# Computing 64 instead of 32 expert tiles of the first table ahead, with the gate matrix built beside 56 of them

## The chip, the core and the metric

The kernel runs on one core of a Trainium2 chip. TensorE (PE) multiplies matrices, VectorE (DVE) and ScalarE (ACT) work element by element, GpSimd (POOL) here starts the row gathers, and SyncE (SP) starts all other transfers. The engines run side by side, each in its own fixed order, and wait for each other by semaphores. The metric is the device time of one launch in microseconds (us); the figure shown is the median of a few runs.

## What is computed

One decoder layer on 512 tokens of width 2048, in float32. The first half (two kinds of linear attention, projections, norms) is untouched here. The second half is PEER, a layer of 16384 single-neuron experts, of which each token uses 128:

```
qry = xt @ w_query                     # 8 heads x 256
s1, s2 = qry halves @ sub_keys         # scores against 128 + 128 keys
v1, i1 = top_k(s1, 16); v2, i2 = top_k(s2, 16)
best, pos = top_k(v1[:, None] + v2[None, :], 16)
expert = i1[pos // 16] * 128 + i2[pos % 16]
gate = softmax(best)
hid = gelu(x . u_tab[expert])          # 128 experts of each token
y = sum(gate * hid * v_tab[expert])
out = rmsnorm(h + y)
```

## The kernel before

The kernel splits the 512 tokens. For 352 of them (`TD`) all 16384 experts are computed densely, and a gate matrix that is zero outside the chosen experts picks the right ones. For the other 160 tokens the chosen rows are gathered from both tables: 320 transfers of 128 rows, 1 MB each.

The dense part runs in 128 tiles of 128 experts and 32 groups of 4 tiles:

- **A tile of the first table** (`u_steps`, L1107): two half-tiles of 512 KB are loaded by SP (`wr`), cast by ACT to a high part `wh` (L100), and DVE subtracts to get the low part `wl` (L102, 128x1024). 48 matmuls of 352 columns follow (L239 to L241, into `lin`). DVE multiplies by the norm (`hid`, L1118, 352 columns) and ACT applies Gelu.
- **A group of the second table** (`v_chunk`, L1151): 8 chunks, each with one `wr` load, one `wh`, one `wl` on DVE and 24 matmuls (L1163 to L1165), whose two results DVE adds to `hT` (L1166, 352 columns). So a group has 8 `wl`, 192 matmuls and 16 additions.
- **The weights of a group** (`w_alloc` L1129, `w_make` L1137): the group's piece of the gate matrix is loaded into `gm` (one buffer, 704 KB); for each of the 4 tiles DVE makes `wf` from `hid` and `gm` (L1142), ACT casts it to `wgh`, DVE makes `wgl` (L1144). The next `gm` load can start when the fourth `wf` has read the buffer.
- **The gate matrix** (`gate_block`, L1073) is built in 88 blocks. For every two blocks DVE runs four 128x1024 operations (L1090 to L1093, tiles `oa`, `ob`); each block has 8 small matmuls (L1100) and one copy on ACT. Every 8 blocks, 2 MB go to DRAM (`gd`).
- **The gather** (`gather_steps`, L1198): POOL starts an indirect transfer into `row` (3 buffers). For a row of the first table DVE multiplies and sums (L1218, 128x2048), for a row of the second it multiplies and adds (L1231, 128x2048). There are 160 of each.

The order is written out in `peer` (L839). (1) While the top-16 indices are worked out, 8 tiles are computed and spilled to DRAM (`hidd`). (2) The *gate stage* computes the next `left = 4*NP1 - et` tiles, spills them, and spreads the 88 blocks evenly over them. (3) The *mixed stage* takes the groups from `NP1` on: for each, 4 tiles of the first table are computed in line, beside the 8 chunks of the group before. (4) The *second-table stage* takes the first `NP1` groups: their `hid` comes back from DRAM (L1148), and only chunks of the second table are computed.

The gather is paced by `tick` (L926), called after each tile, and after each quarter of a group's chunks:

```
slots = 4 * (2 * NG - NP1) + EARLY * 4 * NP1 - 16
self.slot += share
want = int(len(self.steps) * min(self.slot / slots, 1.0))
```

A tick in stages 3 and 4 counts 1, in stages 1 and 2 `EARLY`. The scheduler then fixes each engine's order from this text, and may move a step ahead where it finds room.

Of the kernel before, what the change touches and what calls it, by code (L numbers as in the profile page):

```python
# [42 lines left out]
ND = NC_ - 1  # L43
QS = P // EX
SL = P // QS
NP1 = 8
TS = 8
TB = 32
LAG = 8
X1, X2 = 6, 12  # L50
QW, YL, WAIT = 12, 5, 7
RATE_B, RATE_A, OWED = 1.8, 5.0, 6.0
EARLY = 0.2
GSC = 32768.0


# [21 lines left out]
class Kernel:  # L78
# [760 lines left out]
    def peer(self):  # L839
# [4 lines left out]
        with pool("dp") as self.dp:  # L844
            with pool("tr") as self.trp:
                with pool("tk") as self.tk:
# [23 lines left out]
                    with pool("tk2") as self.fp:  # L870
# [3 lines left out]
                        for n, c in enumerate(list(range(ND, NC_)) + list(range(ND))):  # L874
                            self.pick(c)
                            for _ in range(2):
                                self.u_spill(et)
                                et += 1
                                if self.trs:
                                    self.tick(EARLY)  # L880
                                for _ in soft:
                                    pass
                            self.place(c)
                with pool("tk3") as self.fp:
# [4 lines left out]
                    self.gn = 0  # L889
                    left = 4 * NP1 - et  # L890
                    done = 0
                    for n in range(2 * left):
# [7 lines left out]
                        if n % 2:  # L900
                            hid = next(u)
                            nc.sync.dma_start(self.hidd[et // 4, :, et % 4], hid)
                            et += 1
                            self.tick(EARLY)
            with pool("fo") as self.fop, pool("fq") as self.fp:
                order = list(range(NP1, NG)) + list(range(NP1))
                w, wn = None, None
                self.vn = 0
                for n in range(NG + 1):
                    g = order[n] if n < NG else None  # L910
                    self.vtags = ("g", "g", "g", "s") if n < NG - NP1 else ("g", "s", "lin", "g", "lin", "g", "lin")
                    if g is not None:
                        wn = self.w_alloc(g)
                    for e in range(4):
                        if g is not None:
                            self.w_make(*wn, e, self.u_tile(4 * g + e) if g >= NP1 else self.hid_load(g, e))
                            if g >= NP1:
                                self.tick()
# [7 lines left out]
    def tick(self, share=1.0):  # L926

        slots = 4 * (2 * NG - NP1) + EARLY * 4 * NP1 - 16
        self.slot += share
# [416 lines left out]
```

## Time and profile before

| | before |
|---|---|
| median of 3 runs | 3552.33 us (3538.89 to 3554.91) |
| the profiled execution's own time | 3555.49 us |
| its span | 3553.7 us |
| PE busy | 3333.5 us (94%) |
| DVE busy | 2765.4 us (78%) |
| ACT busy | 1206.4 us (34%) |
| bytes read from and written to HBM | 748.73 MB, 38.09 MB |

The span is the time from the first to the last instruction that the trace has; the own time also has what lies around it. Busy shares are averages over stages with different limits, so the stages are read one by one.

### The profile page before, as it was taken

The page shows a single profiled execution, that of the slowest core. Times are in us where ns is not written, and L with a number is a line of the kernel's source. Part 1 is how long each engine was busy: PE and PEld are TensorE (multiplying, and loading weights), DVE is VectorE, ACT ScalarE, POOL GpSimd, SP SyncE. Part 2 cuts the span into 40 slices and gives each one's busy share as a digit, 9 for nine tenths or more (in the row PEclk, how much of TensorE's full clock was granted, in tenths as well). Part 3 has the DMA queues.
Part 4 walks back from the last instruction along what each step waited for, and adds up shares of the span by engine and source line. Part 5 has one row for each costly group of instructions (what it writes and reads, how often), then busy time and mean ns, then how long its engine had stood idle before and what let it go on. Part 6 is the DMA issues. An engine that isn't in the chain of part 4 may idle for free.

```text
span 3553.7 us, 49698 instructions
## 1 busy us (share of the span) xinstructions
PE 3333.5 (94%) x19740; PEld 3091.5 (87%) x19740; DVE 2765.4 (78%) x4095; ACT 1206.4 (34%) x1499; POOL 873.0 (25%) x533
## 2 busy tenths in 40 slices
PE   7889899999999996888899999999999999999997
PEld 5667678888788996888899999999999999999997
DVE  7666654444534679999899999899899999998666
ACT  5333432322332212355433333333233333333334
POOL 4232223333354230000122222222222222321000
PEclk9889989999999998899999999999999999999999
DMA  4232322222432223556699999999999999998553
GB/s 150 75 92 88 89 60 78 84 77 80 141 118 86 64 71 115 204 198 208 244 346 373 368 370 356 350 372 340 356 365 370 366 376 374 370 367 280 180 178 113
DMA packets 228811, 790.08 MB, mean 222 GB/s; under 512 B 29178, under 2 KB 89850, under 8 KB 185762
## 3 DMA queue, kind: packets, MB, share of 16 engines
q1 hardware_dynamic: 182498, 451.35, 37.1%
q0 software_dynamic: 46080, 335.56, 24.6%
q8 instruction: 154, 2.52, 0.3%
q14 instruction: 79, 0.65, 0.1%
HBM read 748.73 MB, written 38.09 MB: 221 GB/s over the span
## 4 chain that ended last, share of the span: by engine, by line
PE 41%; DVE 27%; issue 14%; DMA 12%; ACT 2%; POOL 2%; SPq 0%; DVEq 0%; POOLq 0%; ACTq 0%
PE lin L239 6%; PE lin L241 6%; PE lin L240 6%; DVE wl L102 5%; DMA wr<-v 4%; DMA wr<-u 4%; DMA row<-vn,eidx 2%; DVE row L1218 2%; POOL row L1205 2%; DVE y_nat L1231 2%; DVE hT L1166 2%; PE g L1164 2%; PE g L1165 2%; PE g L1163 2%; ACT wh L100 1%
## 5 line engine op out<-in xcount | busy, mean ns | idle before, releaser
L100 ACT CAST wh<-wr 128x1024 fp32r<-128x1024 f32 x690 | 725.2, 1051 | 1719.5 <-DMA wr<-v 446.1
L241 PE MATMUL lin<-yh,wl 128*128 128x352 f32 x2048 | 674.6, 330 | 69.2 <-DVE wl L102 68.7
L102 DVE TENSOR_TENSOR wl<-wr,wh 128x1024 fp32r<-128x1024 f32 x512 | 624.7, 1223 | 86.5 <-ACT wh L100 83.0
L239 PE MATMUL lin<-yh,wh 128*128 128x352 f32 x2048 | 667.3, 326 | 12.0 <-ACT wh L100 12.0
L240 PE MATMUL lin<-yl,wh 128*128 128x352 f32 x2048 | 668.6, 327 | 0.0
L102 POOL TENSOR_TENSOR wl<-wr,wh 128x1024 fp32r<-128x1024 f32 x178 | 433.1, 2434 | 872.8 <-ACT wh L100 802.9
L241 PEld LDWEIGHTS lin<-yh,wl 128*128 128x128 f32 x2048 | 390.5, 191 | 85.8 <-DVE wl L102 85.4
L1163 PE MATMUL g<-wgh,wh 128*128 128x352 f32 x1352 | 436.3, 323 | 5.3 <-ACT wh L100 5.3
L1164 PE MATMUL g<-wgl,wh 128*128 128x352 f32 x1352 | 440.0, 325 | 0.9 <-DVE wgl L1144 0.9
L1165 PE MATMUL g<-wgh,wl 128*128 128x352 f32 x1352 | 438.9, 325 | 2.0 <-DVE wl L102 2.0
L1205 POOL DMA_INDIRECT row<-un,eidx x160 | 205.4, 1283 | 896.2 <-DVE row L1218 735.8
L239 PEld LDWEIGHTS lin<-yh,wh 128*128 128x128 f32 x2048 | 390.8, 191 | 15.7 <-ACT wh L100 15.7
L240 PEld LDWEIGHTS lin<-yl,wh 128*128 128x128 f32 x2048 | 389.9, 190 | 0.0
L239 PE MATMUL lin<-xh,wh 128*128 128x512 f32 x912 | 381.3, 418 | 8.6 <-ACT xh L766 8.4
L241 PE MATMUL lin<-xh,wl 128*128 128x512 f32 x912 | 373.4, 410 | 4.5 <-POOL wl L102 4.5
L240 PE MATMUL lin<-xl,wh 128*128 128x512 f32 x912 | 375.1, 411 | 2.6 <-DVE xl L767 2.4
L1205 POOL DMA_INDIRECT row<-vn,eidx x160 | 202.2, 1264 | 591.6 <-DVE y_nat L1231 353.5
L1231 DVE SCALAR_TENSOR_TENSOR y_nat<-row,ww,y_nat 128x2048 f32<-128x2048 f32 x128 | 300.6, 2348 | 0.6 <-DMA row<-vn,eidx 0.2
L1218 DVE SCALAR_TENSOR_TENSOR row<-row,hn_nat 128x2048 f32<-128x2048 f32 x128 | 292.1, 2287 | 3.9 <-DMA row<-un,eidx 3.9
L1163 PEld LDWEIGHTS g<-wgh,wh 128*128 128x128 f32 x1352 | 255.0, 189 | 6.2 <-ACT wh L100 6.2
L1165 PEld LDWEIGHTS g<-wgh,wl 128*128 128x128 f32 x1352 | 254.9, 189 | 2.9 <-DVE wl L102 2.9
L1164 PEld LDWEIGHTS g<-wgl,wh 128*128 128x128 f32 x1352 | 254.6, 188 | 1.2 <-DVE wgl L1144 1.2
(348 smaller groups left out, 5634.2 us busy)
## 6 DMA issues: line engine op xcount, KB each, us to landing
wr<-u SPq DMA_DIRECT2D x256, 512.0 KB
wr<-v SPq DMA_DIRECT2D x256, 512.0 KB
wr<-wi SPq DMA_DIRECT2D x114, 512.0 KB
gd<-st SPq DMA_DIRECT2D x11, 2048.0 KB
gm<-gd SPq DMA_DIRECT2D x32, 704.0 KB
wr<-wo SPq DMA_DIRECT2D x32, 512.0 KB
wr<-wq SPq DMA_DIRECT2D x32, 512.0 KB
hidd<-hid SPq DMA_DIRECT2D x32, 176.0 KB
```

The costliest lines, as they stand in the source:

```text
L100: nc.scalar.copy(hi, raw)
L102: (eng or nc.gpsimd).tensor_tensor(lo, raw, hi.bitcast(F32), op=ALU.subtract)
L239: mm(ps, hi, self.xh[:, k], start=first, stop=False)
L240: mm(ps, hi, self.xl[:, k], start=False, stop=False)
L241: mm(ps, lo, self.xh[:, k], start=False, stop=last)
L1163: nc.tensor.matmul(ps, hv[:, e, sl], wh[:, e], start=(e == 0), stop=False)
L1164: nc.tensor.matmul(ps, hv[:, e, sl], wl[:, e], start=False, stop=False)
L1165: nc.tensor.matmul(ps, lv[:, e, sl], wh[:, e], start=False, stop=(e == 3))
L1166: nc.vector.tensor_tensor(self.hT[:, dt], self.hT[:, dt], ps, op=ALU.add)
L1205: ins = nc.gpsimd.indirect_dma_start(out=r, out_offset=None, in_=self.a[tab], in_offset=bass.IndirectOffsetOnAxis(ap=idx, axis=0))
L1218: nc.vector.scalar_tensor_tensor(r, r, 1.0, hn, op0=ALU.mult, op1=ALU.mult, accum_out=ww[:, i:i + 1])
L1231: nc.vector.scalar_tensor_tensor(y, r, ww[:, i:i + 1], y, op0=ALU.mult, op1=ALU.add)
```

## The change

Two constants are changed:

```
-NP1 = 8
+NP1 = 16
-EARLY = 0.2
+EARLY = 0.4
```

By `NP1`, 64 tiles instead of 32 are computed ahead and spilled: 8 in stage 1 as before, 56 instead of 24 in the gate stage. The mixed stage has 16 groups instead of 24, the second-table stage 16 instead of 8. By `EARLY` a tick in the gate stage counts twice as much, and `slots` becomes 201.6 instead of 214.4. The instructions of PE, DVE, ACT and POOL stay the same in number; SP gets 32 more spills and 32 more loads of 176 KB.

Of the gather's 320 multiplications on DVE, the order of before has 4 ahead of the 8th `hid`, 4 in the gate stage (to the 32nd `hid`), 312 from there to the 128th `hid`, and none in the second-table stage. The order of the change has 4, then 54 in the gate stage (to the 64th), 205 to the 128th, and 57 in the second-table stage, in its first 12 or 13 groups.

DVE in the gate stage, from one tile's `hid` to the next. Before (`oa`, `ob` are the gate blocks' tiles, `wl` the low part of a half-tile):

```order
L1118 TENSOR_TENSOR hid_12052<-lin_11964,rstd 128x352
L1093 TENSOR_TENSOR oa_1941_12055<-oa_1941_12055,tr_11838 128x1024
L1090 TENSOR_TENSOR oa_1951_12116<-iota_10794,tr_11838 128x1024
L1091 TENSOR_TENSOR ob_12118<-iota_10794,tr_11838 128x1024
L1092 TENSOR_TENSOR oa_1952_12117<-oa_1951_12116,tr_11838 128x1024
L102 TENSOR_TENSOR wl_12147<-wr_12143,wh_12145 128x1024
L1093 TENSOR_TENSOR oa_1951_12116<-oa_1951_12116,tr_11838 128x1024
L1090 TENSOR_TENSOR oa_1960_12176<-iota_10794,tr_11838 128x1024
L1091 TENSOR_TENSOR ob_12178<-iota_10794,tr_11838 128x1024
L1092 TENSOR_TENSOR oa_1961_12177<-oa_1960_12176,tr_11838 128x1024
L102 TENSOR_TENSOR wl_12209<-wr_12205,wh_12207 128x1024
L1118 TENSOR_TENSOR hid_12173<-lin_12084,rstd 128x352
```

The same place of the changed kernel (`row` is a gathered row):

```order
L1118 TENSOR_TENSOR hid_11851<-lin_11780,rstd 128x352
L1091 TENSOR_TENSOR ob_11986<-iota_10797,tr_10868 128x1024
L102 TENSOR_TENSOR wl_11958<-wr_11954,wh_11956 128x1024
L1092 TENSOR_TENSOR oa_1920_11985<-oa_1919_11984,tr_10868 128x1024
L1218 SCALAR_TENSOR_TENSOR row_12394,ww_10125<-row_12394,hn_nat 128x2048
L1093 TENSOR_TENSOR oa_1919_11984<-oa_1919_11984,tr_10868 128x1024
L102 TENSOR_TENSOR wl_12005<-wr_12001,wh_12003 128x1024
L1118 TENSOR_TENSOR hid_11936<-lin_11858,rstd 128x352
```

Per tile there are three gate operations and one gather multiplication where there were eight gate operations.

DVE in the second-table stage, from the fourth `wf` that reads one `gm` buffer to the first that needs the next. Before:

```order
L1142 SCALAR_TENSOR_TENSOR wf_27927<-hid_27925,gm_27684 128x352
L1166 TENSOR_TENSOR hT<-hT,g_27714 128x352
L102 TENSOR_TENSOR wl_27812<-wr_27808,wh_27810 128x1024
L1166 TENSOR_TENSOR hT<-hT,s_27734 128x352
L1144 TENSOR_TENSOR wgl_27687<-wf_27850,wgh_27686 128x352
L1144 TENSOR_TENSOR wgl_27687<-wf_27927,wgh_27686 128x352
L1166 TENSOR_TENSOR hT<-hT,lin_27748 128x352
L1142 SCALAR_TENSOR_TENSOR wf_28011<-hid_28009,gm_28005 128x352
```

The changed kernel, in the same stage:

```order
L1142 SCALAR_TENSOR_TENSOR wf_26737<-hid_26735,gm_26494 128x352
L1231 SCALAR_TENSOR_TENSOR hn_nat<-row_27534,ww_10126,hn_nat 128x2048
L1166 TENSOR_TENSOR hT<-hT,s_26558 128x352
L1166 TENSOR_TENSOR hT<-hT,lin_26590 128x352
L102 TENSOR_TENSOR wl_26665<-wr_26661,wh_26663 128x1024
L1166 TENSOR_TENSOR hT<-hT,g_26604 128x352
L1144 TENSOR_TENSOR wgl_26497<-wf_26737,wgh_26496 128x352
L102 TENSOR_TENSOR wl_26699<-wr_26695,wh_26697 128x1024
L1166 TENSOR_TENSOR hT<-hT,lin_26624 128x352
L1142 SCALAR_TENSOR_TENSOR wf_26820<-hid_26818,gm_26814 128x352
```

Between the two `wf` stand one `wl` and five operations of 352 columns before, two `wl`, five of 352 columns and one gather multiplication now.

## Rows read from the trace of the kernel before

**Rows 1.** Page: span, and GB/s moved in 40 equal slices of it.

```profile
span 3553.7 us, 49698 instructions
...
GB/s 150 75 92 88 89 60 78 84 77 80 141 118 86 64 71 115 204 198 208 244 346 373 368 370 356 350 372 340 356 365 370 366 376 374 370 367 280 180 178 113
```

**Rows 2.** Windows by stage: busy us (instructions) per engine, granted clock, DMA share, GB/s.

```profile
core 0: us, PE busy (x) PEld busy (x) DVE busy (x) ACT busy (x) POOL busy (x), PEclk, DMA share, GB/s
1461.00:1742.00 281.00, 244.80 (x1854) 228.14 (x1854) 274.40 (x269) 145.10 (x162) 5.85 (x5) 0.96 0.57 201
1742.00:1850.00 108.00, 101.20 (x616) 99.41 (x616) 92.67 (x97) 34.84 (x44) 26.91 (x20) 0.97 0.93 343
1850.00:3250.00 1400.00, 1369.76 (x8434) 1359.01 (x8435) 1329.64 (x1415) 456.49 (x546) 365.62 (x289) 1.00 0.96 363
3250.00:3534.00 284.00, 283.90 (x1758) 280.64 (x1756) 189.06 (x294) 105.97 (x140) 0.00 (x0) 1.00 0.55 167
```

**Rows 3.** Tile hid: loads and spills, with first and last start (us).

```profile
L1148 SPq DMA_DIRECT2D hid<-hidd x32: 319/326/1653, 3243.3 to 3455.1; - x32
L902 SPq DMA_DIRECT2D hidd<-hid x24: 319/327/424, 1471.2 to 1742.8; - x24
```

**Rows 4.** Lines of DVE, 1461 to 1742 us: count, busy us, mean ns.

```profile
L102 DVE TENSOR_TENSOR wl<-wr,wh 128x1024 fp32r<-128x1024 f32 x47 | 57.1, 1223 | 0.0
...
L1090 DVE TENSOR_TENSOR oa<-iota,tr 128x1024 f16<-128x1024 f16 x44 | 53.8, 1224 | 1.2 <-ACT tr L1070 1.2
```

**Rows 5.** Timeline of DVE in the gate stage: start us, duration us.

```profile
1602.27 1.22 DVE L102 TENSOR_TENSOR wl<-wr,wh 128x1024 fp32r<-128x1024 f32 x1
1603.41 0.52 DVE L1118 TENSOR_TENSOR hid<-lin,rstd 128x352 f32<-128x352 f32 x1
1603.84 1.22 DVE L1093 TENSOR_TENSOR oa<-oa,tr 128x1024 f16<-128x1024 f16 x1
```

**Rows 6.** Lines of DVE, 1850 to 3250 us.

```profile
L102 DVE TENSOR_TENSOR wl<-wr,wh 128x1024 fp32r<-128x1024 f32 x352 | 429.6, 1222 | 61.8 <-ACT wh L100 58.9 <-issue 2.0
L1231 DVE SCALAR_TENSOR_TENSOR y_nat<-row,ww,y_nat 128x2048 f32<-128x2048 f32 x116 | 272.4, 2348 | 0.6 <-DMA row<-vn,eidx 0.2
L1218 DVE SCALAR_TENSOR_TENSOR row<-row,hn_nat 128x2048 f32<-128x2048 f32 x112 | 255.6, 2287 | 0.0
...
L1218 DVE SCALAR_TENSOR_TENSOR row<-row,hn_ex 128x2048 f32<-128x2048 f32 x32 | 73.1, 2288 | 4.2 <-DMA row<-un,eidx 4.2
L1231 DVE SCALAR_TENSOR_TENSOR hn_nat<-row,ww,hn_nat 128x2048 f32<-128x2048 f32 x31 | 72.8, 2348 | 0.1
```

**Rows 7.** Timeline of PE in the gate stage.

```profile
1600.37 0.32 PE L241 MATMUL lin<-yh,wl 128*128 128x352 f32 x1
1600.53 0.32 PE L239 MATMUL lin<-yh,wh 128*128 128x352 f32 x1
...
1605.44 0.62 PE L1100 MATMUL s<-ob,oa 128*128 128x128 f16 x8
1605.90 0.28 PE L1100 MATMUL g<-ob,oa 128*128 128x128 f16 x2
```

**Rows 8.** Window of four groups of the second-table stage, columns as in Rows 2.

```profile
3280.00:3404.00 124.00, 124.00 (x772) 124.00 (x771) 82.63 (x129) 40.12 (x50) 0.00 (x0) 1.00 0.60 183
```

**Rows 9.** Timeline: three `gm` loads and the `wf` that needs each.

```profile
1787.66 0.38 SPq L1132 DMA_DIRECT2D gm<-gd  x1
...
1796.84 0.53 DVE L1142 SCALAR_TENSOR_TENSOR wf<-hid,gm 128x352 f32<-128x352 f32 x1 [3.42 <-DMA gm<-gd]
...
1909.28 0.44 SPq L1132 DMA_DIRECT2D gm<-gd  x1
...
1922.76 0.52 DVE L1142 SCALAR_TENSOR_TENSOR wf<-hid,gm 128x352 f32<-128x352 f32 x1
...
3283.59 0.38 SPq L1132 DMA_DIRECT2D gm<-gd  x1
...
3289.49 0.53 DVE L1142 SCALAR_TENSOR_TENSOR wf<-hid,gm 128x352 f32<-128x352 f32 x1 [1.99 <-DMA gm<-gd]
```

## The prediction

> **What bounds the kernel now.** I began with the transfer rates of the page: up to slice 20 they lie mostly under 200 GB/s, from slice 22 to 36 at 335 to 377, and in the last three under 181 [rows 1]. So the stages have different limits. I cut the execution at the events of the order: the spills of the gate stage start from 1471 to 1743 us, the reloads of the second-table stage from 3243 us [rows 3]. The windows between them are the base of everything below [rows 2].
>
> - Gate stage, 1461 to 1742: 281 us for 24 tiles. DVE is busy for 274.4 of them, PE for 244.8, the transfers at 201 GB/s. DVE is the bound and PE waits for it.
> - Start of the mixed stage, 1742 to 1850: 108 us.
> - Mixed stage, 1850 to 3250: 1400 us. The 352 `wl` of it are 22 groups of 16 [rows 6], so 63.6 us a group. PE and DVE are both at 95% or more, the transfers at a share of 0.96 and 363 GB/s. Three limits lie within a few per cent of each other.
> - Second-table stage, 3250 to 3534: 9 groups in 284 us; four of them took 124 us, 31.0 each, with PE busy without a break and DVE for 82.6 us [rows 8]. PE is the bound; DVE has a third of its time free, and the transfers are at half.
>
> **Unit costs.** A record of DVE overlaps the next one, so I take start to start. A 128x1024 operation costs 1602.27 to 1603.41, 1.14 us; one of 352 columns 0.43 us [rows 5]. The gate operations have the same record as `wl`, 1224 and 1223 ns [rows 4], so also 1.14. A gather multiplication has a record of 2.29 or 2.35 us [rows 6]; with the same overlap of 0.085 us taken off, and the short read of the sum that follows L1218 added, both cost about 2.27. Check on a mixed group: 16 x 1.14 + 28 x 0.43 + 13.3 x 2.27 (292 multiplications in 22 groups) = 60.5 us; measured 1329.64 / 22 = 60.4. A matmul of 352 columns costs 0.161 us on PE (124.00 us / 772 in [rows 8], and 1600.37 to 1600.53 in [rows 7]), a gate matmul 0.46 / 8 = 0.058 [rows 7].
>
> **The change stage by stage.** No operation of PE, DVE, ACT or POOL is added; time can only come from better or worse overlap.
>
> 1. Gate stage. Before, DVE had 47 `wl`, 24 `hid`, 175 gate operations and 4 multiplications: 53.6 + 10.3 + 199.5 + 9.1 = 272.5 us, and the stage took 281, 1.024 times the busy time of 274.4. PE needed 1152 x 0.161 + 704 x 0.058 = 226 us: 55 us of PE were lost. Now there are 56 tiles: DVE 112 x 1.14 + 56 x 0.43 + 176 x 1.14 + 54 x 2.27 = 475 us; PE 2688 x 0.161 + 41 = 474 us. Both are full at once. The nearest rows for that are the mixed groups: 63.6 us against PE's 384 x 0.161 = 61.8, 1.029. The other end is the start of the mixed stage: 8 tiles and one group need 92.7 us of PE, and took 108, 1.165 (with new buffers, and transfers at 0.93). I take 1.028, 488 us; the ends are 475 and 553. The bytes (56 half-tile pairs, 11 stores, 54 rows of 1 MB, spills) are about 148 MB in 488 us, 304 GB/s, under the 363 of the mixed stage. The 32 more spills are 5.8 MB, hidden by the same margin; should that cover go, they cost 5.8 MB at 363 GB/s, 16 us. On SP a spill waits for its `hid`, and the loads behind it wait with it; in the order of the change, 5 half-tiles are issued ahead of it beyond its own tile, some 20 us of PE, so I put this at nothing.
> 2. Start of the mixed stage: 108 us again (20 multiplications before, 21 now).
> 3. Mixed stage: 14 groups between the same marks, not 22. They carry 13.3 multiplications each, as before: 14 x 63.6 = 891 us; 882 to 903 if each group moves by 0.6 to 0.9.
> 4. Second-table stage: 17 groups, not 9. The last 4 to 5 have no gather and cost 31.0; 5 us of the 284 are beyond 9 x 31.0, and stay. The first 12.5 carry 57 multiplications, 4.5 each. DVE then needs 8 x 1.14 + 24 x 0.43 + 4.5 x 2.27 = 29.7 us a group of PE's 31.0: its free third is gone. And DVE waits here for `gm`. Alone, the load takes 5.9 us from issue to the `wf` that waits for it, 1.99 of them as DVE idle time; beside the gather it took 9.2 with 3.42 idle; and a `wf` 13.5 us after the issue did not wait [rows 9]. So under gather it lands after 9.2 to 13.5 us. The changed order puts only 6.7 to 8.7 us of DVE's work between the release of the buffer and the next need (13.5 or more in the mixed stage), 7.2 at the median. The wait is 2.0 to 6.3 us a group; below nothing it can't go, since an early landing leaves PE's 31.0 as the floor. I take 3.0, near the low end, because the load of 9.2 is the only one under gather that was itself waited for in these rows and the rate here is lower than in the mixed stage. With 2.7% on DVE's own 29.7 as in the gate stage: 33.5 us a group. Behind the waiting `wf` in DVE's queue stand the `wl` that PE waits for, so the wait reaches PE. 12.5 x 33.5 + 4.5 x 31.0 + 5 = 563 us. The ends: 31.0 a group, 532 us; and 36.8 (29.7 x 1.027 + 6.3), 605.
>
> The Trainium skill, "DMA: Bandwidth & Descriptors", section "Queues, rings and completion order", says that each transfer engine takes turns between the queues that have work, a packet at a time. The 5.9 against 9.2 us agrees in kind: SP's queue, which carries `gm`, loses turns to POOL's gather. By that rule with equal turns, `gm` and one `wr` ahead of it (1.25 MB) at half of 377 GB/s take some 6.6 us, an estimate from rates in [rows 1]; the wait would vanish and the stage would cost 12.5 x 31.0, 30 us less. The row of 9.2 speaks against so short a load.
>
> **Sum.** Before 281 + 108 + 1400 + 284 = 2073 us; now 488 + 108 + 891 + 563 = 2050. That is 23 less. The profiled execution took 3555.5 us, of which 3553.7 is span; it lies 3.2 above the median of 3552.3. Against that median I predict 3552.3 - 23, about 3529 us.
>
> **Rivals.**
>
> - *The second-table stage stays on PE.* `gm` lands within DVE's work and the groups take 31.0: 12.5 x 2.5 = 31 us less, about 3498. For it: the transfers need about 10.4 MB a group, some 335 GB/s, less than in the mixed stage. Against it: DVE waited for `gm` even at 183 GB/s [rows 8, 9].
> - *PE and DVE stall on each other in the gate stage.* With no slack on either, each wait of one is a wait of both. At 1.10, between the two nearest rows, the stage takes 522 us, 34 more than I forecast: 3563, no change. For it: the clock. The stage had a granted mean of 0.96, so part of it at 1.2 instead of 2.4 GHz, while PE idled between pieces; if it stays so, PE's 474 becomes 494 before any stall. Against it: in the mixed stage, where PE was busier, the clock is 1.00.
> - *The gather beside the second table costs more than it saves: slower.* Place: DVE, at the first `wf` of each group. Price: `gm` at its upper bound of 13.5 us is a wait of 6.3 us, and as SP issues it among the chunks' loads, these fall behind too; 37.5 us a group is 12.5 x 4.0 = 50 us more, 3579. It decides from 36.8 us a group on, where the loss passes 18 us above before. For it: one buffer, and half of the cover that the mixed stage has. Against it: at that pace the transfers fall to 280 GB/s, and the load gets quicker.
>
> **Chances.** Forecast 0.44 (its own range 3511 to 3547), second-table stage on PE 0.23, gate stage coupled 0.18, slower 0.15. About 0.5%, 18 us, is what a measurement here can tell from no change: faster is under 3534.6, slower over 3570. The forecast lies 6 us under the first mark, so 0.66 of it is faster and 0.34 is the same. Faster: 0.23 + 0.29 = 0.52. Same: 0.15 + most of the coupled case, 0.15, is 0.30. Slower: 0.15 and 0.03 of the coupled case, 0.18. For 8 in 10 the range runs from a little under the second case, 3492, to just over the mark of slower, 3572.
>
> **What will show it.** In the profile after: the gate stage's window at 488 us from the 8th to the 64th spill, with PE near 97% and a granted clock of 1.00; a mixed group at 63.6 us; the second-table groups at 33.5 us while L1231 and L1218 still run and at 31.0 after. DVE's waits for `gm` should be about 3 us each, some 12 times. The prediction is wrong if the gate stage takes over 510 us, or if the second-table groups with gather stay at 31 or pass 36.

## The result, and the profile of the changed kernel

The changed kernel takes 3528.8 us (median of 20 runs, 3510.9 to 3551.2), the kernel before 3552.8 in the runs made beside it. The ratio is 0.9937, with a 95% interval of 0.9918 to 0.9956: faster, by about 24 us. The forecast was 3529. That it agrees so closely is luck: three terms were off by 11 to 23 us and cancelled.

The page of the changed kernel answers to [rows 1]. The high stretch now begins at the 18th slice, near 300 GB/s, where before the rate was about 200 until the 19th; only the last two slices are low.

```profile
span 3534.2 us, 49832 instructions
...
GB/s 147 76 96 88 83 64 81 78 81 78 130 130 85 71 66 120 209 293 292 277 318 294 316 346 375 370 368 355 358 360 365 372 366 333 349 322 335 332 183 111
```

The spills and reloads answer to [rows 3]: 64 tiles go out and come back, 8 of them ahead of the gate stage.

```profile
L1148 SPq DMA_DIRECT2D hid<-hidd x64: 319/357/3013, 2964.6 to 3435.4; - x64
L902 SPq DMA_DIRECT2D hidd<-hid x56: 319/327/327, 1468.8 to 1966.7; - x56
```

The same windows as in [rows 2], cut by these marks, with the same columns: gate stage, start of the mixed stage, mixed stage, second-table stage with gather, and that stage without.

```profile
1459.00:1966.00 507.00, 488.26 (x3417) 473.60 (x3417) 476.66 (x444) 230.19 (x261) 90.97 (x54) 0.98 0.79 289
1966.00:2085.00 119.00, 99.10 (x590) 97.93 (x589) 91.87 (x101) 32.67 (x41) 23.99 (x21) 0.91 0.89 333
2085.00:2975.00 890.00, 870.65 (x5364) 863.21 (x5364) 846.15 (x898) 293.57 (x351) 239.67 (x186) 1.00 0.96 365
2975.00:3384.00 409.00, 402.57 (x2488) 400.56 (x2487) 381.59 (x500) 130.11 (x158) 49.77 (x53) 1.00 0.91 323
3384.00:3515.00 131.00, 130.43 (x805) 127.16 (x803) 85.00 (x132) 56.52 (x81) 0.00 (x0) 1.00 0.44 135
```

Cut at the same instructions in both traces, and set against what PE alone needs (0.161 us a matmul of 352 columns, so 31.0 us a second-table group, and 41 us for the gate matmuls), the stages are:

| stage | before | PE's need | lost | forecast | after | PE's need | lost |
|---|---|---|---|---|---|---|---|
| gate stage | 280 | 226 | 54 | 488 | 507 | 474 | 33 |
| start of mixed | 108 | 93 | 15 | 108 | 119 | 93 | 26 |
| mixed | 1400 | 1360 | 40 | 891 | 889 | 865 | 24 |
| second table | 284 | 279 | 5 | 563 | 540 | 527 | 13 |
| sum | 2072 | 1958 | 114 | 2050 | 2055 | 1959 | 96 |

PE's need is the same, as no work was added. What fell is PE's lost time, by 18 us; the span fell by 19.5. The loss in the gate stage is now spread over 56 tiles instead of 24, and eight fewer mixed groups each lose 1.8 us.

**Where the gate stage loses its 33 us.** The waits of the stage (what waited, for what: us in all, times, longest) in the changed kernel:

```profile
ACT wh L100 <- DMA wr<-u: 49.4, 19, 10.8
...
ACT st L1102 <- DMA gd<-st: 31.9, 8, 9.1
DVE wl L102 <- ACT wh L100: 24.1, 11, 5.5
```

One such place, first SP, then ACT, then DVE (start us, duration us, and the idle time ahead in brackets):

```profile
1594.02 0.33 SPq L1104 DMA_DIRECT2D gd<-st  x1
```

```profile
1608.75 1.10 ACT L1102 COPY st<-g 128x512 f32<-128x512 f32 x1 [9.07 <-DMA gd<-st]
1612.01 1.04 ACT L100 CAST wh<-wr 128x1024 fp32r<-128x1024 f32 x1 [2.17 <-DMA wr<-u]
```

```profile
1613.09 1.23 DVE L102 TENSOR_TENSOR wl<-wr,wh 128x1024 fp32r<-128x1024 f32 x1 [5.50 <-ACT wh L100]
```

The 2 MB store of the gate matrix is issued at 1594. The next copy into `st` may not start before it has left, at 1608.75. In ACT's queue the cast of a half-tile stands behind that copy, and the half-tile itself is late too. So DVE idles 5.5 us, and PE 2.8 us behind it. The windows of the 15 us after this store and after the next, with the time between them, show the transfer engines (second column from the right, as a share) full while a store runs, and with much to spare else:

```profile
1594.00:1609.00 15.00, 15.00 (x110) 14.60 (x109) 13.59 (x12) 2.85 (x4) 4.49 (x2) 1.00 0.99 364
1609.00:1640.00 31.00, 28.19 (x198) 26.85 (x197) 26.91 (x22) 16.37 (x20) 4.49 (x4) 1.00 0.73 265
1641.00:1656.00 15.00, 10.94 (x50) 10.36 (x50) 12.62 (x11) 3.07 (x4) 3.55 (x3) 0.77 1.01 389
```

The mean of 289 GB/s over the stage hides this. A half-tile load issued in the third of these windows takes 11.5 us, on the chain of waits (start us, us, what):

```profile
1651.22 11.51 DMA wr<-u
...
1663.92 0.56 PE lin L239
1664.48 0.29 PE lin L241
...
1667.88 0.16 PE lin L241
```

PE has waited 3 us for it, and then runs its next matmuls at 0.29 us, the 1.2 GHz level (granted 0.72 from 1664 to 1670), before it is back at 0.16. The stage's 33 us are thus 507 - 488 = 19 us of idle PE and 488 - 474 = 14 us more under busy matmuls. Of these 14, 3 also stand in the runs below in which the clock is 1.00 (477 busy); much of the rest is the lower clock (granted mean 0.98).

### The profile page after: what moved, and what is told of

Its sections match the earlier page's. It is cut to its first block, busy times and chain, and to the rows that moved or that the text cites. A ratio compares the mean times of both kernels' runs of the same rounds, so it can differ in the third digit from the quotient of the medians.

```text
span 3534.2 us, 49832 instructions
## 1 busy us (share of the span) xinstructions
PE 3323.9 (94%) x19740; PEld 3085.3 (87%) x19740; DVE 2760.3 (78%) x4095; ACT 1206.8 (34%) x1499; POOL 878.8 (25%) x533
## 4 chain that ended last, share of the span: by engine, by line
PE 51%; DVE 19%; issue 14%; DMA 12%; POOL 2%; ACT 1%; SPq 0%; DVEq 0%; POOLq 0%; ACTq 0%
PE lin L239 8%; PE lin L241 7%; PE lin L240 7%; DMA row<-vn,eidx 3%; DVE wl L102 3%; DMA wr<-u 3%; PE g L1165 2%; PE g L1164 2%; PE g L1163 2%; POOL row L1205 2%; PE lin L1165 2%; PE lin L1164 2%; PE lin L1163 2%; DVE row L1218 2%; DMA wr<-v 1%
## 5 line engine op out<-in xcount | busy, mean ns | idle before, releaser
L1165 PE MATMUL g<-wgh,wl 128*128 128x352 f32 x1188 | 384.9, 324 | 3.5 <-DVE wl L102 3.3
L1164 PE MATMUL g<-wgl,wh 128*128 128x352 f32 x1188 | 385.4, 324 | 0.0
L1163 PE MATMUL g<-wgh,wh 128*128 128x352 f32 x1188 | 382.4, 322 | 2.3 <-ACT wh L100 2.3
L1165 PEld LDWEIGHTS g<-wgh,wl 128*128 128x128 f32 x1188 | 223.3, 188 | 5.5 <-DVE wl L102 5.4
L1163 PEld LDWEIGHTS g<-wgh,wh 128*128 128x128 f32 x1188 | 223.5, 188 | 2.6 <-ACT wh L100 2.6
L1164 PEld LDWEIGHTS g<-wgl,wh 128*128 128x128 f32 x1188 | 223.2, 188 | 0.0
```

Source lines behind the costliest of these rows:

```text
L1163: nc.tensor.matmul(ps, hv[:, e, sl], wh[:, e], start=(e == 0), stop=False)
L1164: nc.tensor.matmul(ps, hv[:, e, sl], wl[:, e], start=False, stop=False)
L1165: nc.tensor.matmul(ps, lv[:, e, sl], wh[:, e], start=False, stop=(e == 3))
```

## The experiments

The two ideas that they were to tell apart first: in the gate stage PE and DVE stall on each other because both are full (the second rival of the prediction), or the transfers are late there.

**Which of the two constants does it.** All edits are against the changed kernel.

```
-EARLY = 0.4
+EARLY = 0.2
```

> 64 tiles ahead, EARLY left at 0.2 (slots becomes 188.8). The orders of all engines differ from the changed kernel's in under 2% of the places on any engine, and the gather multiplications stand 54 / 206 / 56 in the gate stage, mixed stages and second-table stage as there. Theory (the number of tiles does it all, the gather goes where DVE has room whatever EARLY says): the same time as the changed kernel, 0.994 of before. Rival (the larger share of the gather, set by EARLY, brings part of the gain): half of it is gone, 0.997 or more, and a longer second-table stage than 540 us.

Measured: 0.9944 [0.9924, 0.9964], the same as the change. In the gate stage stand 54 gather multiplications as without the edit, and the stage takes 509 us. The number of tiles does it all: in the two traces the orders hardly differ (31 of DVE's 3935 operations stand elsewhere, none of POOL's), so the scheduler brings the gather forward whichever pace is asked for.

```
-NP1 = 16
+NP1 = 8
```

> 32 tiles ahead, EARLY 0.4. The order has 12 gather multiplications in the gate stage instead of 4. Theory: the gate stage is bound by DVE there, so it gets 8 x 2.27 = 18 us longer (299 us), the mixed groups lose 8 multiplications of 292 and gain up to 1400 x 8 / 292 x 0.5 = some 19 us: 1.000 of before within 0.3%. Rival (the mixed stage is bound by the gather, and each multiplication taken out of it counts in full, while DVE in the gate stage takes them in its gaps): 0.995.

Measured: 1.0093 [1.0057, 1.0129], slower than the kernel before, which neither idea expected. The gate stage, in the trace of this run:

```profile
1462.00:1765.00 303.00, 254.52 (x1850) 237.71 (x1848) 291.75 (x283) 143.88 (x162) 18.05 (x13) 0.92 0.59 213
```

Beside [rows 2] DVE has 17.4 us more to do (8 more multiplications at 2.27 us are 18) and the stage is 22 us longer: where DVE bounds, gather work moved in is paid in full, and the granted clock falls from 0.96 to 0.92. The mixed stage gave nothing back: 63.5 us a group, with 8 multiplications fewer in it. If DVE were its limit, it would have given back 18 us. So DVE was not.

**A second buffer for the gate piece `gm`.**

```
-        gm = self.ft("gm", (P, nb, 4, TB))
+        gm = self.ft("gm", (P, nb, 4, TB), bufs=2)
```

> The changed kernel with two buffers for gm. Theory (DVE's waits for the gate matrix's piece reach PE): the two waits of 8.2 and 9.3 us at the start of the mixed stage and the 6.9 us at the start of the second-table stage go, the start takes 102 to 108 us instead of 119; 15 to 22 us less than the changed kernel, 0.988 to 0.990 of before. Rival (the transfers are the bound there, and an earlier load only takes the others' turns): the same as the changed kernel, 0.994.

Measured: 0.9901 [0.9872, 0.9930], 3516.5 us. The start of the mixed stage falls from 119 to 110 us, the second-table stage from 540 to 530 (its first group from 36 to 32), the gate stage stays at 507. The start in its trace, clock 0.97 instead of 0.91:

```profile
1966.00:2076.00 110.00, 97.79 (x584) 95.94 (x583) 92.19 (x101) 32.02 (x40) 23.83 (x22) 0.97 0.98 367
```

**The gate stage without the gather.** The first run leaves out the gather altogether, transfers and multiplications:

```
-            for b in range(slots // 16):
-                for i in range(16 * b, 16 * b + 16):
-                    steps.append(lambda i=i, f=up: f(i))
...
```

> The changed kernel without the gather: no rows of the two tables are loaded, and their multiplications and the Gelu between are left out, so 160 tokens lack their expert part. DVE then needs 351 us in the gate stage, PE still 474. Theory of the prediction (the gate stage's 507 us are PE and DVE both full, stalling each other): 480 to 485 us. Rival (the 2 MB stores of the gate matrix, which hold up the copies into the one st buffer and the half-tile loads behind them): 495 us or more. The mixed groups should come to PE's 61.8 to 62.2 us from 63.6, the second-table groups to 31.0.

Measured in one run: 3456.8 us, the gate stage 477. The second run keeps DVE's multiplications but not the transfers; all of them read one row tile that stays in place:

```
-            r = self.gp.tile([P, D], F32, tag="row", name=self.nm("row"), bufs=3)
-            ins = nc.gpsimd.indirect_dma_start(
...
+            return still
```

> The changed kernel with the gather's multiplications but without its transfers: every multiplication reads one row tile that is loaded once, so the 160 gathered tokens come out without meaning. DVE's order has 53 multiplications in the gate stage, 188 in the mixed stages, 67 in the second-table stage; DVE still needs some 472 us in the gate stage and PE 474. Theory of the prediction (the 30 us above PE's time are DVE and PE both full, each wait of one a wait of both): 498 to 507 us. Rival (the gather's transfers share the engines with the 2 MB stores and the half-tile loads, which come late; with DVE full but transfers free there is little loss): 478 to 486 us. Mixed groups: 63.5 by the first, 62 by the second.

Measured in one run: 3437.9 us. The gate stage in its trace:

```profile
1454.00:1931.00 477.00, 477.00 (x3406) 465.55 (x3405) 475.55 (x443) 230.73 (x260) 0.00 (x0) 1.00 0.57 189
```

PE is busy for all 477 us and DVE for 475.6 of them, at a clock of 1.00. Two engines that are both full lose almost nothing here (477 against PE's 474), so the idea that they stall on each other falls. The loss needs the gather's transfers. The start of the mixed stage takes 94 us in this trace and a mixed group 61.6, PE's own time, so the losses there need them too. Without them the half-tiles also land sooner. From issue to landing (least, median, most) in the gate stage of the changed kernel:

```profile
DMA to landing us min/median/max: 3.3/5.3/17.1
```

and of the kernel with multiplications only:

```profile
DMA to landing us min/median/max: 3.4/3.7/8.4
```

**Are the 2 MB stores part of it?** One run gives them to ACT's queue, so that on SP no half-tile stands behind a store:

```
-                nc.sync.dma_start(self.gd[c * (P // TB) + tb], st)
+                nc.scalar.dma_start(self.gd[c * (P // TB) + tb], st)
```

> The changed kernel with the 11 stores of the gate matrix started by ACT instead of SP, so that half-tile loads do not stand behind 2 MB in SP's queue. Theory (loads of up to 11 us behind a store make PE wait): the gate stage falls from 507 to 485 to 495 us, 0.989 to 0.991 of before. Rival (all transfers share the same engines, and the copy into the one st buffer still waits for the store): 500 us or more, 0.993 to 0.995.

Measured: 0.9978 [0.9955, 1.0000], slower than the change. The gate stage takes 521 us. Its waits in that trace, beside 49.4 and 31.9 above:

```profile
ACT wh L100 <- DMA wr<-u: 60.1, 18, 9.7
...
ACT st L1102 <- DMA gd<-st: 27.0, 6, 8.8
```

So it isn't the order in SP's queue: beside the store as behind it the half-tiles are late. The other run leaves the stores out and loads the gate pieces from an input table instead:

```
-        self.gd = tc.dram_tile([TD // TB, P, P, TB], F32, name="gd")
+        self.gd = a["un"][0:2 * P * (TD // TB)].rearrange("(b p x) (y t) -> b p (x y) t", p=P, x=2, t=TB)
...
-                nc.sync.dma_start(self.gd[c * (P // TB) + tb], st)
+                pass
```

> The changed kernel without the 11 stores of the gate matrix: the matrix is built in SBUF as before, and the pieces of it are loaded from another tensor of the same shape in DRAM, so the expert part of the 352 dense tokens has no meaning. Since the gate stage without the gather's transfers took 477 us (PE's own 474) and with them 507, one theory is that the stores and the gather together delay the copies into the one st buffer and the loads behind a store: without stores the gate stage takes 477 to 485 us. Rival: the gather alone delays the half-tile loads (8.6 us from issue to cast at the median, with 3 buffers), and the stage stays at 495 to 507 us.

Measured in one run: 3507.3 us. Gate stage and half-tile loads in its trace:

```profile
1463.00:1942.00 479.00, 477.90 (x3408) 465.92 (x3407) 476.00 (x443) 231.45 (x261) 87.64 (x54) 1.00 0.74 261
```

```profile
DMA to landing us min/median/max: 3.4/4.6/11.2
```

479 us with the gather but no store, 477 with the stores but no gather, 507 with both. Either alone leaves the stage within 3 to 5 us of PE's need; together they cost some 30 us. In the run without the gather the 15 us after a store leave the transfer engines a quarter of their time:

```profile
1605.00:1620.00 15.00, 15.00 (x110) 14.60 (x109) 11.40 (x12) 6.59 (x8) 0.00 (x0) 1.00 0.78 281
```

So the cause is the 2 MB stores together with the gather's 1 MB rows. But not every store costs time. Ten of the eleven have their 15 us within the stage of the changed kernel, and the transfer engines' share is 0.96 or more in each of them; yet 13 of PE's 19 idle us follow two stores, issued at 1641 and 1832, and none follow five others. What sets the two apart in the trace are the gather's rows: in the 18 us from 8 us before the store, POOL works on five rows there, and on two or three around each of the others. POOL's row starts around the store at 1641 and around one that costs nothing (busy us and count, granted clock, share, GB/s):

```profile
1632.80:1650.80 18.00, 5.95 (x5) 0.89 0.97 364
1914.60:1932.60 18.00, 1.87 (x2) 1.00 1.00 384
```

All engines from a store to the next, first after the two that cost most, then after that one:

```profile
1641.00:1693.00 52.00, 44.95 (x289) 43.17 (x289) 45.14 (x39) 20.66 (x24) 6.36 (x4) 0.90 0.74 270
1832.10:1880.00 47.90, 41.91 (x289) 40.83 (x288) 44.23 (x42) 21.14 (x24) 7.27 (x4) 0.93 0.80 292
1922.60:1965.20 42.60, 42.60 (x306) 41.54 (x305) 41.82 (x35) 21.10 (x23) 12.50 (x6) 1.00 0.83 297
```

In the traces with `EARLY` at 0.2 and with two `gm` buffers the same two stores, again with five rows around them, are followed by 5.6 to 7.9 us of idle PE each. No run moves the rows away from the stores, so that their number decides is read from the traces and not tested.

**A fourth half-tile buffer.** If late loads are the loss, more of them in flight should hide it. Room comes from the second `tr` buffer.

```
+        self.wc = getattr(self, "wc", -1) + (eng is not None)
+        if eng is not None and self.wc % 4 == 3:
+            raw = self.ft("wr", (P, 8, P))
...
-        tr = self.ft("tr", (P, 4, P), F16, bufs=2)
+        tr = self.ft("tr", (P, 4, P), F16, bufs=1)
```

> The changed kernel with a fourth buffer for the half-tile loads in all stages after the scores (and one tr buffer instead of two, to make room). The order takes 57 multiplications into the gate stage instead of 54. Theory (a half-tile's buffer is held for the load of 8.6 us, the cast of 1.05, a wait of 2.0 and the subtraction of 1.14; 12.8 us over 3 buffers is 4.3 us a half-tile where PE wants 4.24 in the gate stage and 3.86 in the mixed stage): with 4 buffers the gate stage falls to 482 to 492 us and a mixed group to 62.0 to 62.6; 0.984 to 0.988 of before. Rival (the transfers' rate is the bound, a fourth load in flight only makes each slower): gate 500 or more, mixed 63.5, 0.993 to 0.995.

Measured: 0.9856 [0.9832, 0.9880], 3496.4 us. The gate stage falls to 494 us, the start of the mixed stage rises to 125, the second table stays at 539, and the mixed stage falls to 863:

```profile
2073.00:2936.00 863.00, 861.66 (x5366) 860.96 (x5365) 844.50 (x902) 291.06 (x347) 237.65 (x186) 1.00 0.98 376
```

That is 61.6 us a group, as in the run without the gather's transfers, and PE is busy for all but 1.3 us. ACT's waits for half-tiles in the mixed stage were, in the changed kernel,

```profile
ACT wh L100 <- DMA wr<-v: 280.4, 98, 10.2
ACT wh L100 <- DMA wr<-u: 150.8, 58, 5.7
```

and are with four buffers

```profile
ACT wh L104 <- DMA wr<-u: 31.6, 11, 8.2
ACT wh L104 <- DMA wr<-v: 26.3, 12, 3.9
```

though a load takes no less time, first in the changed kernel and then with four buffers:

```profile
DMA to landing us min/median/max: 3.6/7.4/13.9
```

```profile
DMA to landing us min/median/max: 3.8/7.8/14.8
```

A half-tile is needed every 3.85 us (61.6 / 16), so three buffers allow 11.6 us from the issue of a load to the `wl` that frees the buffer. 7.4 of load, 1.05 of cast and 1.14 of `wl` leave 2 us at the median and nothing for a load of 13.9; four buffers allow 15.4. Without the gather's transfers the loads of the mixed stage land in 3.6 us at the median, and three buffers are enough.

**The fourth buffer up to the gate stage only, with two `gm` buffers.**

```
...
+        if eng is not None and not hasattr(self, "fop") and self.wc % 4 == 3:
...
+        gm = self.ft("gm", (P, nb, 4, TB), bufs=2)
```

> The changed kernel with a fourth buffer for the half-tile loads up to the end of the gate stage only, and two buffers for gm. Theory: the gate stage as with four buffers throughout (482 to 492 us), the start of the mixed stage and the second-table stage as with two gm buffers (110 and 530 us); 0.984 to 0.986 of before. Rival: the gate stage stays at 500 or more and the kernel is as fast as with two gm buffers alone, 0.990.

Measured: 0.9918 [0.9893, 0.9943], 3521.9 us. In total that is no faster than two `gm` buffers alone, as the rival had it, although the gate stage takes 493 us, as the theory had it. The start takes 111 us and the second table some 530, but a mixed group 64.4. As `tr` has one buffer here too, this also shows that the mixed stage's gain is the fourth buffer's. Why its groups are slower than the 63.5 of the change is not explained.

**More tiles ahead**, each with two `gm` buffers:

```
-NP1 = 16
+NP1 = 24
```

> 96 tiles ahead (NP1 = 24) with two buffers for gm. The order has 124 multiplications in the gate stage (DVE 720 us, PE 88 x 7.73 + 41 = 721), 100 in the mixed stages, 92 in the second-table stage. Theory (the loss of the gate stage comes with the 11 stores and is shared by more tiles, and a mixed group loses 1.8 us that a tile ahead and a second-table group do not): gate 750, first group 110, 6 mixed groups 381, second-table stage 783, a span of some 3503 us, 0.987 of before. Rival (each tile in the gate stage loses the same 0.54 us as in the changed kernel, whatever the stores do): gate 768 or more, no better than 64 tiles with two gm buffers, 0.990.

Measured: 1.0023 [0.9997, 1.0050], 3562.0 us, against 3516.5 for 64 tiles with two `gm` buffers. That is the rival's side, and beyond its 0.990. The gate stage in its trace, of an execution of 3542.4 us, 20 below the median:

```profile
1443.00:2237.00 794.00, 748.80 (x4972) 729.87 (x4971) 720.99 (x642) 311.88 (x359) 162.90 (x125) 0.97 0.87 326
```

88 tiles in 794 us, 9.0 each, as at 56 tiles; PE needs 721 of it. The loss more than doubles, from 33 to 73 us. The gather stands denser here, 124 multiplications beside 88 tiles against 54 beside 56, and ACT waits 134 us for half-tiles against 49. How the added loss divides between the stores and the three buffers is not tested. And with `NP1 = 32`, all tiles ahead and no mixed stage:

> All 128 tiles ahead (NP1 = 32), so no mixed stage, with two buffers for gm. The order has 194 multiplications in the gate stage (DVE 967 us, PE 120 x 7.73 + 41 = 969) and 122 in the second-table stage. Theory: gate 994, second-table stage with its start 1018, a span of some 3490 us, 0.984 of before. Rival (the gather at 1.6 rows a tile brings the transfers to 0.95 and the gate stage loses 3% or more as the mixed stage does): gate 1000 to 1040, 0.987 to 0.995.

Measured: 1.0075 [1.0046, 1.0103], 3581.6 us, slower than before, where both ideas expected a gain. The gate stage takes 1068 us for 120 tiles, 8.9 each.

**Both edits everywhere.** The fourth half-tile buffer in all stages and two `gm` buffers, with room from one `tr`, one `wf` and a narrower square buffer:

```
...
+        sq = acc if first else (self.ft("t_sq", bufs=2)[:, 0:n] if n > TD else self.ft("t_sv", (P, TD)))
...
-        w = self.ft("wf", (P, TD), bufs=2)
+        w = self.ft("wf", (P, TD), bufs=1)
```

> The changed kernel with a fourth half-tile buffer in all stages after the scores and two gm buffers; to make room, one tr, one wf and one 352-column buffer for the last squares instead of two each. If the two effects add (the fourth buffer: gate stage 507 to 494, mixed group 63.5 to 61.6; the second gm: start of the mixed stage 125 to 112, second-table stage 539 to 530): a span of some 3472 to 3482 us, 0.979 to 0.982 of before. If they don't (with PE the bound in the mixed stage already, and the single wf putting DVE's and ACT's steps for the four tiles in a row): 0.984 to 0.987, as with the fourth buffer alone.

Measured: 0.9828 [0.9801, 0.9856], 3496.5 us. It beats both kernels, the changed one by some 32 us by the medians. Its four stages:

```profile
1465.00:1959.00 494.00, 481.55 (x3400) 468.45 (x3399) 482.32 (x443) 230.38 (x260) 90.64 (x56) 0.99 0.82 303
1959.00:2078.00 119.00, 96.24 (x587) 95.25 (x586) 99.72 (x108) 33.75 (x44) 25.61 (x25) 0.90 0.96 365
2078.00:2949.00 871.00, 866.98 (x5392) 865.04 (x5391) 846.13 (x904) 293.90 (x349) 234.94 (x186) 1.00 0.97 374
2949.00:3475.00 526.00, 525.65 (x3278) 522.09 (x3277) 454.72 (x617) 187.29 (x237) 43.25 (x46) 1.00 0.77 267
```

The second table is at PE's own pace, but the start stays at 119 us and the mixed groups are at 62.2. In the start one cast of ACT comes after a wait of 16.1 us and PE idles 22.4 us behind it; why that wait is there is not settled. The two edits add up only in part, and against the fourth buffer alone the intervals overlap.

## Why the prediction was right, and where it was not

- **The total and its cause: right, its exactness luck.** No work was added; PE fills in what DVE's gate work left idle. Lost PE time fell by 18 us; 23 was forecast.
- **Gate stage, 488 us by "1.028": too small by 19.** DVE's 475 us were right (476.7 measured), and so were PE's 474. The ratio was taken from the mixed groups, which have the gather but no 2 MB store, and lose their 1.8 us to the three half-tile buffers; the stage has both, and together they cost 30 us (507 against 479 and 477). The term was mis-sized, not for want of slack between PE and DVE, as the second rival had it. Its 522 us were reached only with the stores on ACT's queue.
- **"The 32 more spills ... hidden": agrees.** With the spills in place but without gather or without stores, the stage stands within 3 to 5 us of PE's need.
- **Start of the mixed stage, 108: too small by 11.** DVE waits twice for `gm`, 8.2 and 9.3 us. Before it waited 2.93 us for the first load (issued at 1755.72, read at 1768.10) and 3.42 for the second, which is the one in [rows 9]. The two loads, and the first one of the second-table stage:

```profile
1979.92 0.38 SPq L1132 DMA_DIRECT2D gm<-gd  x1
2015.33 0.51 SPq L1132 DMA_DIRECT2D gm<-gd  x1
...
2969.30 1.40 SPq L1132 DMA_DIRECT2D gm<-gd  x1
```

```profile
1995.12 0.53 DVE L1142 SCALAR_TENSOR_TENSOR wf<-hid,gm 128x352 f32<-128x352 f32 x1 [8.16 <-DMA gm<-gd]
...
2031.00 0.53 DVE L1142 SCALAR_TENSOR_TENSOR wf<-hid,gm 128x352 f32<-128x352 f32 x1 [9.28 <-DMA gm<-gd]
...
2981.67 0.97 DVE L1142 SCALAR_TENSOR_TENSOR wf<-hid,gm 128x352 f32<-128x352 f32 x2 [6.89 <-DMA gm<-gd]
```

  From issue to read the loads took 15.2, 15.7 and 12.4 us. With a second buffer the start took 110 us, 9 of the 11 less. The first load also waits for the last store, which writes what it reads: SP stands 12.2 us before it, 3.9 in the kernel before. Without the stores the start took 110 us too, though the loads still took 15.0 us at the median; without the gather's transfers it took 94. So the excess needs the gather, and the last store and the one buffer both have a part in it. Why the loads at this place are slower than in the trace before isn't settled.
- **Mixed groups at 63.6 us: right (63.5), for a wrong reason.** "Three limits lie within a few per cent" was read from three high shares. Neither DVE (less gather changed nothing) nor the rate (376 GB/s with four buffers) was the limit: it was the time that a half-tile needs through three buffers, under the gather's transfers.
- **Second-table groups, 33.5 us by "I take 3.0": too large, 23 us in the stage.** After the first one, the 13 `gm` loads land like this in the changed kernel, with DVE's idle time for them:

```profile
  DMA gm<-gd: 2.1, 3
...
DMA to landing us min/median/max: 5.9/6.8/7.8
```

  So the load lands in 7 us under gather, not in 9.2 to 13.5. The 13 groups took 409 us, 36 the first and 31.1 on average the others: the first rival's mechanism, which has a floor of 31.0. The row of 9.2 came from the start of the mixed stage, at 343 GB/s; the stage that it was used for runs at 323. By the prediction's own mark ("stay at 31") this step is wrong. The turns between queues of the Trainium skill, "DMA: Bandwidth & Descriptors", section "Queues, rings and completion order", gave the prediction its estimate of 6.6 us for this load (at 377 GB/s, where [rows 1] has 376 at most). This stage agrees (6.8), the 15.2 and 15.7 us at the start of the mixed stage do not.
- **The sum.** +19 + 11 - 2 - 23 = +5 against the forecast of these stages; the rest of the two executions differs by 2 us the other way.

## What to carry to other kernels

Where a stage is bound by one engine and another stage by a second one, work of the second put beside the first pays only until both are full; here 64 tiles are the best of the numbers tried, and 32 more gave it all back. A mean rate over a stage hides where large transfers meet; set the start times of stores and gathered rows side by side. High busy shares of three resources don't name the limit: look at how long one buffer is held (load, cast, read) against the pace at which buffers are needed, and try one buffer more. A latency should be taken from a stage with the same traffic; one row from a stage's start mis-sized the second-table stage by 23 us.

## What the runs showed of the hardware that was not expected

- DVE and PE were both full at once, 475.6 and 477.0 of 477 us, and lost 3 us against PE's 474.
- The 2 MB stores alone left the gate stage at 477 us, the gather's 1 MB rows alone at 479. Together they filled the transfer engines after a store (share 0.96 to 1.01) and lengthened half-tile loads to as much as 17.1 us, in a stage that moves 289 GB/s on average. Full engines alone did not stop PE: it lost 6 and 7 us after the two stores with five rows around them, and nothing after five of the others.
- Moving the stores from SP's queue to ACT's went with longer waits for half-tiles (60.1 us against 49.4) and a stage 14 us slower.
- A gap on PE cost more than itself: after one of 3 us the next matmuls took 0.29 us instead of 0.16, and stretches with such gaps have a granted mean of 0.90 to 0.98.
